# Key pages and new key rows transposed by VectorE in 32x32 blocks, decode rows ordered by groups of four heads

## The chip, the cores and the metric

The kernel runs on one core of a Trainium2 chip. The metric is the device time of one execution in microseconds (us); a time is the median of several runs on the same chip.

## The reference

One inference step of a decoder trunk with two layers. Layer 0 is a conformer convolution, layer 1 is stick-breaking attention; a gated ConvFFN follows each, and a final RMSNorm ends the trunk. There are 512 prompt rows (one new sequence) and 32 decode rows (8 sequences of 4 new tokens). The model width is 1024, in 16 heads of 64. Everything is float32. Each decode sequence has a past of 256 keys and values, which lie in two pages of 128 rows each in a pool of pages; a page table names them. What the change touches is the attention:

```python
def stick_breaking_block(q, k, v, bias, q_start):
    z = jnp.einsum('bqhd,bkhd->bhqk', q, k) * (HEAD_DIM ** -0.5) + bias[None, :, None, None]
    valid = k_pos[None, :] < q_pos[:, None]
    log_fail = jnp.where(valid, jax.nn.log_sigmoid(-z), 0.0)
    after = lax.cumsum(log_fail, axis=3, reverse=True) - log_fail
    weights = jnp.where(valid, jnp.exp(jax.nn.log_sigmoid(z) + after), 0.0)
    return jnp.einsum('bhqk,bkhd->bqhd', weights, v)
...
k_past = jnp.take(cache_k[a], page_table, axis=0)   # 8 sequences x 2 pages x 128 rows x (16 heads x 64)
v_past = jnp.take(cache_v[a], page_table, axis=0)
```

The new keys and values of both prompt and decode rows are outputs as well, one row per token (k_p and v_p for the prompt, k_s and v_s for the decode rows).

## The kernel before

Activations lie transposed in SBUF: 128 channels on the partitions, 8 blocks c of channels, 544 columns (512 prompt rows, then 32 decode rows). Each block holds two heads, one on partitions 0 to 63 and one on 64 to 127. A weight matrix comes in as float32 (raw) and is split into two parts, whi by ScalarE (L398) and wlo by VectorE (L401); activations are split into XH and XL; a product is three matmuls, XH by whi, XL by whi and XH by wlo (in the attention stage L2126, L2127 and L2128). They are called weight matmuls here. In SBUF and PSUM the names are: acc, z, dz, av, one and t are PSUM tiles, the rest is in SBUF.

In the attention stage, about 634 to 834 us of the profile's span, the key and value projections of layer 1 run channel block by channel block (`keys(c, h)` and `values(c, h)`, in two halves h of the columns), and around them goes the attention work of prompt and decode rows. All of it is entered into a list scheduler (`Plan`): each operation is entered with its engine, a cost from a table and what it reads and writes, ranks follow from these, and the scheduler writes out the order of each engine once, when the program is built. On the chip each engine then works through its own order, and waits where an input or a buffer isn't there. When a step moves to another engine or gets another cost, the order around it changes too.

The steps that the change touches:

- **Key pages.** `gather` (L2018): GpSimd issues an indirect DMA per page, 128 rows of 4 KB. Sixteen key pages are gathered and then, into the same buffers, sixteen value pages. The first three are requested before the stage. In `page_logits(m)`, for four pages at a time (m = 0 to 3), PE transposes each page in two groups of four blocks (L2246, into PSUM); one group is copied to SBUF by VectorE, the other by ScalarE (L2253). Pages of the first sequence go into kt, a part of kT's tile, those of the second into two e tiles (`second`).
- **Page logits** (L2264). The decode queries lie in Qz, with two heads in one block of 128 rows (a block-diagonal layout) and 32 columns for each sequence; per m there are 16 matmuls, 32 rows of output by 256 keys. A decode row in these tiles is one of a group g of eight heads.
- **New keys** (`keys`). ScalarE copies the projection into kT (L2164, which also fills kT_s, the decode rows' keys); PE transposes two 128-column blocks per half (L2156), VectorE copies them to kr (L2170), SP stores kr (L2171) in runs of 512 bytes. kr has two buffers. `values` uses the same L2156 for vT.
- **Placing the decode queries.** GpSimd copies qT's decode columns into Qz (L2044, `place_q`, for four sequences at a time) and Qf (L2050), 64 partitions at a time: 2 + 2 and 4 copies.
- **New logits** (L2282): the decode queries Qf by the new keys kT_s, 16 matmuls of 32 by 32. `new_rows` (L2194) transposes the decode rows of k and v for their outputs.
- **Values.** `sequence(n)` (L2326) multiplies the weights of one sequence by its two value pages, 16 matmuls of 32 by 128; the result is added into oacc. `new_values(bg)` adds the new values (L2346, two matmuls of 128 by 128) and transposes oacc (L2351) into dec, the attention output of the decode rows.
- **Prompt attention** uses L2388 (logits), L2394 to L2422 (weights, with scans on VectorE, L2418, and masks on GpSimd, L2402), L2430 and L2450.

SP issues the weight loads and most other DMAs, in one queue in program order.

Of the kernel before, what the change touches and what calls it, by code (L numbers as in the profile page):

```python
# [9 lines left out]
F32 = mybir.dt.float32  # L10
# [240 lines left out]
def tile_trunk(  # L251
# [181 lines left out]
    mnew = base.tile([P, 2, NS], F32, name="mnew")  # L433
    bcol = base.tile([P, 2], F32, name="bcol")
    own = base.tile([P, 4], F32, name="own")
# [4 lines left out]
    oh = base.tile([P, 2, H], F32, name="oh")  # L440
    cb = base.tile([P, 2, NS], F32, name="cb")
    m1 = base.tile([P, NS], F32, name="m1")
    rb = base.tile([P, 2], F32, name="rb")
# [204 lines left out]
    def decode_tables():  # L648
# [6 lines left out]
        dve.tensor_scalar(ti[:, 0:1], pid, 3, 3, op0=ALU.logical_shift_right, op1=ALU.bitwise_and)  # L655
        dve.tensor_scalar(ti[:, 1:2], pid, 3, None, op0=ALU.bitwise_and)
        dve.tensor_scalar(ti[:, 2:3], pid, 5, None, op0=ALU.logical_shift_right)
        dve.tensor_scalar(ti[:, 3:4], pid, 2, 1, op0=ALU.logical_shift_right, op1=ALU.bitwise_and)
        dve.tensor_copy(ti[:, 4:5], pid)
        dve.tensor_copy(tf[:, 0:5], ti[:, 0:5])  # L660
        dve.scalar_tensor_tensor(tf[:, 5:6], tf[:, 2:3], 2.0, tf[:, 3:4], op0=ALU.mult, op1=ALU.add)
        dve.tensor_scalar(cb_i[:, 0, :], t32, 2, None, op0=ALU.logical_shift_right)
# [1918 lines left out]
```

## Time and profile before

| | before |
|---|---|
| median of 3 runs | 1266.06 us (1265.24 to 1266.23) |
| the profiled execution: its own time | 1266.66 us |
| its span | 1265.0 us |
| TensorE clock granted | 0.999 |

The profile is one execution. The span is what the profiler saw from the first to the last instruction, and 1.66 us of the execution's own time lie around it. PE is TensorE's matmuls, PEld its weight loads (they overlap PE), DVE VectorE, ACT ScalarE, POOL GpSimd, SP SyncE; a q behind an engine's name is that engine's DMA issuing. Busy time counts instructions at work; an engine's wait counts only between its instructions. One fp32 matmul shows as two records on PE. Durations of matmuls overlap, since PE is pipelined: what one occupies is read from the distance between starts. A timeline row gives the start in us, the duration, the engine, the line, the operation with its output and inputs, the shapes, and how many instructions stand in the row. A row of a group gives, behind the bar, busy us, mean ns of one, and then the idle time of the engine just before them with what ended it.

### The profile page before, as it was taken

The numbers are of one execution on the slowest core, as the hardware profiler recorded it, in microseconds if no ns is written. First come the engines' busy times: TensorE is split into PE (matmuls) and PEld (weight loads), VectorE is DVE, ScalarE is ACT, GpSimd is POOL, SyncE is SP. The second block draws the span as 40 slices with busy tenths as digits, with TensorE's granted clock in tenths as the row PEclk, the third lists the DMA queues.
The fourth block names the chain that finished last, engine by engine and source line by source line (L and its number), as shares of the span: only waits on it lengthen the run. The fifth ranks groups of instructions, "written<-read, shape, count | busy, mean of one in ns | idle before, by whom it ended". The sixth has DMA issues, their size and how long they took to land.

```text
span 1265.0 us, 26475 instructions
## 1 busy us (share of the span) xinstructions
PE 1253.8 (99%) x10846; PEld 1203.5 (95%) x10846; DVE 1004.6 (79%) x1696; ACT 717.2 (57%) x1436; POOL 165.6 (13%) x291
## 2 busy tenths in 40 slices
PE   9999999999999999999999999999999999999998
PEld 8997699999999999999989888999999999999997
DVE  7999886988987887869865589766988987887863
ACT  6794584646645455445565498754645645454453
POOL 5000014111001000002042143200111001000000
PEclk9999999999999999999999999999999999999999
DMA  7465423123233233244355544342223233232221
GB/s 215 127 172 151 128 68 116 34 85 118 92 98 114 67 119 105 71 144 171 117 183 152 157 139 137 114 148 71 65 87 110 84 110 117 67 118 88 89 77 72
DMA packets 119179, 142.39 MB, mean 113 GB/s; under 512 B 5101, under 2 KB 110245, under 8 KB 118786
## 3 DMA queue, kind: packets, MB, share of 16 engines
q1 hardware_dynamic: 110350, 111.89, 28.4%
q0 software_dynamic: 8704, 28.80, 7.2%
q8 instruction: 85, 1.39, 0.5%
q14 instruction: 36, 0.29, 0.1%
q10 hardware_dynamic: 4, 0.01, 0.0%
HBM read 129.34 MB, written 12.18 MB: 112 GB/s over the span
## 4 chain that ended last, share of the span: by engine, by line
PE 84%; DVE 13%; ACT 1%; issue 1%; DMA 0%; DVEq 0%; ACTq 0%
PE acc L1632 5%; PE acc L1631 5%; PE acc L1630 5%; PE acc L756 4%; PE acc L757 4%; PE acc L758 4%; PE av L893 3%; PE av L1409 3%; PE av L1410 3%; PE av L1411 3%; DVE wlo L401 3%; PE tr L1410 3%; PE tr L1409 3%; PE tr L1411 3%; PE tr L1630 3%; PE tr L1632 2%
## 5 line engine op out<-in xcount | busy, mean ns | idle before, releaser
L398 ACT CAST whi<-raw 128x1024 fp32r<-128x1024 f32 (+2 forms) x247 | 224.2, 911 | 119.4 <-PE av L1410 24.9
L401 DVE TENSOR_TENSOR wlo<-raw,whi 128x1024 fp32r<-128x1024 f32 (+2 forms) x247 | 259.2, 1052 | 26.1 <-ACT whi L398 24.8
L756 PE MATMUL acc<-XH,whi 128*128 128x288 f32 (+1 forms) x384 | 112.7, 294 | 0.0
L758 PE MATMUL acc<-XH,wlo 128*128 128x288 f32 (+1 forms) x384 | 110.3, 287 | 0.9 <-DVE wlo L401 0.9
L757 PE MATMUL acc<-XL,whi 128*128 128x288 f32 (+1 forms) x384 | 110.3, 287 | 0.0
L1409 PE MATMUL av<-HH,whi 128*128 128x288 f32 (+1 forms) x280 | 83.2, 297 | 0.4 <-DVE xT L1719 0.4
L1410 PE MATMUL av<-HL,whi 128*128 128x288 f32 (+1 forms) x280 | 82.6, 295 | 0.0
L1632 PE MATMUL acc<-TH,wlo 128*128 128x272 f32 x288 | 82.6, 287 | 0.0
L1631 PE MATMUL acc<-TL,whi 128*128 128x272 f32 x288 | 82.6, 287 | 0.0
L1630 PE MATMUL acc<-TH,whi 128*128 128x272 f32 x288 | 82.6, 287 | 0.0
L2126 PE MATMUL acc<-XH,whi 128*128 128x256 f32 (+1 forms) x264 | 82.0, 310 | 0.6 <-ACT kT L2164 0.6
L1411 PE MATMUL av<-HH,wlo 128*128 128x288 f32 (+1 forms) x280 | 82.2, 294 | 0.0
L1666 ACT COPY G<-acc 128x272 f32<-128x272 f32 (+1 forms) x72 | 26.8, 372 | 93.9 <-PE acc L1632 93.9
L1409 PE MATMUL tr<-HH,whi 128*128 128x256 f32 (+1 forms) x280 | 78.6, 281 | 0.0
L1410 PE MATMUL tr<-HL,whi 128*128 128x256 f32 (+1 forms) x280 | 78.4, 280 | 0.0
L1411 PE MATMUL tr<-HH,wlo 128*128 128x256 f32 (+1 forms) x280 | 78.3, 280 | 0.0
L2128 PE MATMUL acc<-XH,wlo 128*128 128x256 f32 (+1 forms) x264 | 75.8, 287 | 0.0
L2127 PE MATMUL acc<-XL,whi 128*128 128x256 f32 (+1 forms) x264 | 75.7, 287 | 0.0
L756 PEld LDWEIGHTS acc<-XH,whi 128*128 128x128 f32 x384 | 72.2, 188 | 1.4 <-issue 0.4
L758 PEld LDWEIGHTS acc<-XH,wlo 128*128 128x128 f32 x384 | 72.1, 188 | 1.1 <-DVE wlo L401 1.1
L757 PEld LDWEIGHTS acc<-XL,whi 128*128 128x128 f32 x384 | 72.2, 188 | 0.3
L1570 DVE SCALAR_TENSOR_TENSOR cv<-G,fprm,cv 128x560 f32<-128x560 f32 x88 | 69.5, 797 | 0.5
(465 smaller groups left out, 4373.8 us busy)
## 6 DMA issues: line engine op xcount, KB each, us to landing
raw<-in_ffn_w_gate_dram SPq DMA_DIRECT2D x22, 1024.0 KB
raw<-in_ffn_w_up_dram SPq DMA_DIRECT2D x22, 1024.0 KB, 5.4
raw<-in_ffn_w_down_dram SPq DMA_DIRECT2D x24, 768.0 KB, 4.6
raw<-in_attn_w_qkv_dram SPq DMA_DIRECT2D x12, 1024.0 KB, 5.3
raw<-in_conv_w_in_dram POOLq DMA_DIRECT2D x6, 1024.0 KB, 6.9
rep<-glu SPq DMA_DIRECT2D x36, 142.0 KB, 2.9
raw<-in_conv_w_out_dram POOLq DMA_DIRECT2D x4, 1024.0 KB, 6.0
raw<-in_ffn_w_down_dram SPq DMA_DIRECT2D x8, 512.0 KB
```

What stands on the lines that cost most here:

```text
L398: act.copy(hi[:, k, :], src[:, k])
L401: dve.tensor_tensor(lo[:, k, :], src[:, k], hi[:, k, :], op=ALU.subtract)
L756: pe.matmul(o, hi[:, k, :], XH[:, k, c0:c0 + n], start=(k == 0), stop=False)
L757: pe.matmul(o, hi[:, k, :], XL[:, k, c0:c0 + n], start=False, stop=False)
L758: pe.matmul(o, lo[:, k, :], XH[:, k, c0:c0 + n], start=False, stop=(k == NC - 1))
L1409: pe.matmul(o, hi[:, j + k, :], xh, start=(start and k == 0), stop=False, **kw)
L1410: pe.matmul(o, hi[:, j + k, :], xl, start=False, stop=False, **kw)
L1411: pe.matmul(o, lo[:, j + k, :], xh, start=False, stop=(stop and k == len(xs) - 1), **kw)
L1630: pe.matmul(o, hi[:, j + k, :], xh, start=(start and k == 0), stop=False, **kw)
L1631: pe.matmul(o, hi[:, j + k, :], xl, start=False, stop=False, **kw)
L1632: pe.matmul(o, lo[:, j + k, :], xh, start=False, stop=(k == 3), **kw)
L2126: pe.matmul(o, hi[:, k, :], XH[:, k, c0:c0 + n], start=(k == 0), stop=False)
```

## The change

Key pages and new key rows are no longer transposed on PE. SP now reads the 16 page numbers of the table into registers (`page_numbers`), early in the program, and loads each key page with four DMAs of its own (`key_page`), each with 32 partitions by four runs of 1 KB: partition 32x + p holds, for each quarter q of the page, row 32q + p of the four heads 4x to 4x + 3. One VectorE instruction then transposes the 32x32 blocks of the whole page (128x1024), into kt or an e tile. Value pages stay with GpSimd's indirect DMA. A half of new keys is transposed by one VectorE instruction of 128x256 and stored by four DMAs with runs of 128 bytes.

Channels of key pages stand on the partitions in another order than before: a block k of 32-channel pieces holds one piece of each of the four groups of four heads. So decode rows are ordered by groups of four heads, and everything that meets them changes: Qz becomes 128x1024, GpSimd places queries in sixteen copies of 32 partitions (`place_q`, `place_f`), the new keys' decode columns are copied into the same order (kn, `place_k`, sixteen copies, new), the page logits of the second sequence are 16 matmuls of 128 keys rather than 8 of 256, new logits are two batches of 16 matmuls, the value products 8 matmuls of 256 columns, new values two of 256 columns, and the rows of new keys, new values and the result are turned by matmuls with pieces of the identity. Masks and the logit bias get columns for the new order. The lines of the changed kernel have other numbers: L2145 to L2147 are the weight matmuls, L2282 the page logits, L2264 and L2188 VectorE's transposes, L2417 the prompt's logits, L2061 and L2066 the copies into Qz and Qf, L2296 those into kn, L2431 the masks.

```diff
+            plan.op("sp", 1.0, page_numbers, w=["numbers"])
+            plan.op("dve", 0.6, decode_columns, r=["numbers"], w=["tables"])
+            plan.op("dve", 0.9, decode_masks, r=["tables"])
             for j in range(PAGE_BUFS):
-                plan.op("pool", 1.05, lambda j=j: gather(page_t[j], j, ck), r=["saved", "tables"])
+                plan.op("sp", 2.0, lambda j=j: key_page(page_t[j], j), r=["saved", "numbers"])
...
+    def page_numbers():
+        numbers.extend(nc.sync.value_load(idx[0:1, j:j + 1], min_val=0, max_val=cache_k.shape[1] - 1) for j in range(2 * NB))
+
+    def key_page(t, j):
+
+        pages = cache_k[0, bass.ds(numbers[j], 1)].rearrange("o (q p) (x h) d -> o x p q (h d)", p=32, x=4)
+        for x in range(4):
+            nc.sync.dma_start(out=t[32 * x:32 * x + 32, :].rearrange("p (q r) -> p q r", q=4), in_=pages[0, x])
...
-    Qz = xflat[:, 3 * D:3 * D + NC * 160].rearrange("p (c r) -> p c r", c=NC)
...
-    Qf = dz.tile([P, NC, 2, NS], F32, name="Qf")
+    Qz = xflat[:, 3 * D:4 * D].rearrange("p (k r) -> p k r", k=NC)
+
+    Qf = dz.tile([P, NC, 2 * NS], F32, name="Qf")
     pool.memset(Qz, 0.0)
     pool.memset(Qf, 0.0)
 
...
+    def placed(bg):
+        new = SEQ + 16 * bg
+        for x in range(4):
+            for q in range(4):
+                src = qT[32 * q:32 * q + 32, 2 * x:2 * x + 2, new:new + 16]
+                yield slice(32 * x, 32 * x + 32), x, q, src.rearrange("p c (b i) -> p c b i", b=4)
 
     def place_q(bg):
...
+        for rows, x, q, src in placed(bg):
+            dst = Qz[rows].rearrange("p (c q) (b r) -> p q c b r", q=4, b=4)[:, q, :, :, 4 * x:4 * x + 4]
+            pool.tensor_copy(dst, src)
...
+    def place_f(bg):
+        for rows, x, q, src in placed(bg):
+            dst = Qf[rows].rearrange("p (c q) (b r) -> p q c b r", q=4, b=4)[:, q, :, :, 4 * x:4 * x + 4]
+            pool.tensor_copy(dst, src)
 
     place_q(0)
...
-        rows, src = to_rows(lambda b: kT[:, c, c0 + b * P:c0 + (b + 1) * P], [("k", c, h)])
         kr = sbuf("kr", 2 * P, 2)
-        plan.op("dve", 0.38, lambda: dve.tensor_copy(kr().rearrange("p (b d) -> p b d", b=2), src()), r=[rows], w=[kr])
-        plan.op("sp", 3.0, lambda: nc.sync.dma_start(out=kpv[:, 2 * h:2 * h + 2, c * P:(c + 1) * P],
-                                                     in_=kr().rearrange("p (b d) -> p b d", b=2)), r=[kr])
+        plan.op("dve", 0.15 + 256 * 1.1e-3, lambda: dve.transpose(kr(), kT[:, c, c0:c0 + 256]), r=[("k", c, h)], w=[kr])
+
+        def store():
+            for a in range(4):
+                rows = slice(32 * a, 32 * a + 32)
+                nc.sync.dma_start(out=k_p[0, 0, c0:c0 + 256].rearrange("(b i) h d -> i b (h d)", i=32)[:, :, c * P + 32 * a:c * P + 32 * a + 32],
+                                  in_=kr()[rows].rearrange("i (b j) -> i b j", j=32))
+
+        plan.op("sp", 5.0, store, r=[kr])
...
+            for x in range(4):
+                for j in range(2):
+                    pe.matmul(rows()[HALF[j], x * HD:(x + 1) * HD], src[HALF[j], 2 * x:2 * x + 2, :].rearrange("p c t -> p (c t)"),
+                              ident[HALF[j], HALF[j]], start=(x == 0), stop=(x == 3), skip_group_check=True)
...
+            return t
+        if i < 2 * NB:
+            plan.op("sp", 2.0, lambda: key_page(t(), i), w=[t, ("asked", i)])
         else:
-            plan.op("pool", 1.05, lambda: gather(t(), i % (2 * NB), ck if i < 2 * NB else cv), w=[t, ("asked", i)])
-            plan.op(f"page{i}", 4.0, lambda: None, r=[("asked", i)], w=[(t, 1)])
+            plan.op("pool", 1.05, lambda: gather(t(), i % (2 * NB), cv), w=[t, ("asked", i)])
+        plan.op(f"page{i}", 6.0 if i < 2 * NB else 4.0, lambda: None, r=[("asked", i)], w=[(t, 1)])
...
+                plan.op("pool", 2.4, lambda: place_q(1), w=["Qz"])
         z = zt[bg]
         for odd in range(2):
             for pg in range(2):
                 t = page(4 * m + 2 * odd + pg)
-                for half in range(2):
-                    pt = spare if spare and (odd, pg, half) == (0, 0, 1) else psum("t")
...
-                    def turn(t=t, pt=pt, half=half):
-                        for j in range(4):
-                            c = half * 4 + j
-                            pe.transpose(pt()[:, j * P:(j + 1) * P], t()[:, c * P:(c + 1) * P], ident)
...
-                    plan.op("pe", 0.43, turn, r=[t, (t, 1), "pages"], w=[pt])
-                    eng = ("dve", "act")[half]
...
-                    def keep(pt=pt, half=half, pg=pg, odd=odd, copy=(dve.tensor_copy, act.copy)[half]):
-                        home = second[half]().rearrange("p (c k) -> p c k", c=4) if odd else kt[:, half * 4:half * 4 + 4]
-                        copy(home[:, :, pg * P:(pg + 1) * P], pt().rearrange("p (c k) -> p c k", c=4))
...
-                    plan.op(eng, 0.68 if half == 0 else 0.6, keep, r=[pt], w=[("ktq" if odd else "ktp", 2 * pg + half)],
-                            a=[second[half]] if odd else [])
+
+                def turn(t=t, pg=pg, odd=odd):
+                    dve.transpose(second[pg]() if odd else kt[:, pg * D:(pg + 1) * D], t())
+
+                plan.op("dve", 1.25, turn, r=[t, (t, 1), "pages"], w=[("ktq" if odd else "ktp", pg)],
+                        a=[second[pg]] if odd else [])
 
         def logits():
             for odd in range(2):
                 b = 2 * (m % 2) + odd
...
-        plan.op("pe", 1.72, logits, r=[(k, i) for k in ("ktp", "ktq") for i in range(4)] + ["Qz", *second], w=[z], form="c32")
+                c0 = 32 * b - 16 * odd
+                if odd:
+                    parts = [(pg * P, P, second[pg]()) for pg in range(2)]
+                else:
+                    parts = [(0, KW, kt)]
+                for e in range(2):
+                    for lo, n, src in parts:
+                        keys_of = src.rearrange("p (q k j) -> p k q j", k=NC, j=32)
+                        for u in range(4):
+                            k = 4 * (u % 2) + 2 * (u // 2) + e
+                            pe.matmul(z()[32 * u:32 * u + 32, (m % 2) * KW + lo:(m % 2) * KW + lo + n],
+                                      Qz[:, k, c0:c0 + 32], keys_of[:, k],
+                                      start=(b == e == 0), stop=(b == 3 and e == 1), skip_group_check=True)
...
+    def place_k():
+        for x in range(4):
+            for q in range(4):
+                pool.tensor_copy(kn[32 * x:32 * x + 32].rearrange("p (c q) t -> p q c t", q=4)[:, q], kT_s[32 * q:32 * q + 32, 2 * x:2 * x + 2, :])
+
     def new_logits():
...
+        zn = psum("t")
+        plan.op("pool", 3.0, place_k, r=[("kT_s", c) for c in range(NC)], w=["kn"])
+        for bg in range(2):
+            plan.op("pool", 3.0, lambda bg=bg: place_f(bg), w=["Qf"])
+
+            def f(bg=bg):
+                for v in range(2):
+                    t = 2 * bg + v
+                    for e in range(2):
+                        for u in range(4):
+                            k = 4 * (u % 2) + 2 * (u // 2) + e
+                            pe.matmul(zn()[32 * u:32 * u + 32, t * NS:(t + 1) * NS], Qf[:, k, 32 * v:32 * v + 32], kn[:, k, :],
+                                      start=(t == e == 0), stop=(t == 3 and e == 1), skip_group_check=True)
+
+            plan.op("pe", 0.6, f, r=["Qf", "kn"], w=[zn], form="c32")
...
+            for pg in range(2):
+                values_of = ts[pg]().rearrange("p (x h d) -> p h x d", x=4, h=4)
+                for u in range(4):
+                    pe.matmul(pt()[32 * u:32 * u + 32, :2 * P], wT[:, t, pg, 32 * u:32 * u + 32], values_of[:, 2 * (u % 2) + u // 2],
+                              start=(pg == 0), stop=(pg == 1), skip_group_check=True)
...
+            for v in range(2):
+                pe.matmul(pt()[:, v * KW:(v + 1) * KW], wn[:, 2 * bg + v, :], new_s,
+                          start=(v == 0), stop=True, skip_group_check=True)
 
         def turn():
...
+            first = True
+            for x in range(4):
+                for j in range(2):
+                    for v in range(2):
+                        pick = ident.rearrange("p (j c b x i) -> p j x c b i", j=2, c=2, b=2, x=4)[:, j, x]
+                        home = tr()[HALF[j], :2 * P].rearrange("p (x c v b i) -> p x v c b i", x=4, c=2, v=4, b=2)[:, x, v]
+                        pe.matmul(home, oacc[:, 2 * bg + v, x * HD:(x + 1) * HD], pick, start=(x == v == 0), stop=(x == 3 and v == 1),
...
-        split(hi, lo, dec[rows, :, :, 4 * j:4 * j + 4])
+    split(XH[:, :, SEQ:T], XL[:, :, SEQ:T], dec.rearrange("p c v r -> p c (v r)"))
```

How the orders change, at three places.

PE, in the order before, around the first page logits (L2264; dz is their PSUM tile, xT in L2264 is Qz, kT and the two e tiles hold the transposed pages):

```order
L2246 MATMUL t_8261<-ident,xT 128x128 x4
L2388 MATMUL z_8266<-kT,qT 128x384
L2388 MATMUL z_8268<-kT,qT 128x384
L2388 MATMUL z_8266<-kT,qT 128x128
L2388 MATMUL z_8268<-kT,qT 128x128
L2264 MATMUL dz_8273<-kT,xT 32x256 x8
L2264 MATMUL dz_8273<-e_8192,xT 32x256 x4
L2264 MATMUL dz_8273<-e_8212,xT 32x256 x4
```

And PE in the changed kernel, at its first page logits (L2282):

```order
L2145 MATMUL acc_8411<-XH,whi_8160 128x256
L2146 MATMUL acc_8411<-XL,whi_8160 128x256
L2147 MATMUL acc_8411<-XH,wlo_8161 128x256
L2282 MATMUL dz_8461<-kT,xT 32x256 x8
L2282 MATMUL dz_8461<-e_8324,xT 32x128 x4
L2282 MATMUL dz_8461<-e_8403,xT 32x128 x4
L2282 MATMUL dz_8461<-e_8324,xT 32x128 x4
L2282 MATMUL dz_8461<-e_8403,xT 32x128 x4
```

The page transposes between the weight matmuls are gone, and the page logits stand right behind weight matmuls.

GpSimd before, in the last third of the stage (L2402 are the prompt's masks, L2018 gathers of value pages):

```order
L2402 AFFINE_SELECT e_9882<-e_9882 128x2x128
L2018 DMA xT<-in_cache_v_dram,idx 128x1024
L2402 AFFINE_SELECT e_9988<-e_9988 128x2x128 x2
L2018 DMA xT<-in_cache_v_dram,idx 128x1024 x2
L2402 AFFINE_SELECT e_10204<-e_10204 128x2x128 x2
```

GpSimd in the changed kernel, there:

```order
L2431 AFFINE_SELECT e_9980<-e_9980 128x2x128 x2
L2032 DMA xT<-in_cache_v_dram,idx 128x1024
L2296 COPY kn<-kT_s 32x2x32 x16
L2431 AFFINE_SELECT e_10172<-e_10172 128x2x128 x2
L2066 COPY Qf<-qT 32x2x4x4 x16
L2431 AFFINE_SELECT e_10470<-e_10470 128x2x128
```

The sixteen copies into kn and the second sixteen into Qf come between the masks; the first batch of new logits reads kn, the second reads kn and the second half of Qf.

VectorE before, shortly ahead of the stage (L1490, L1486, L1372 and L1868 belong to the queries' projection):

```order
L1490 TENSOR_TENSOR TLq<-kT,THq 128x2x272 x2
L1868 SCALAR_TENSOR_TENSOR qT<-acc_7815,qT 128x272
L1486 TENSOR_TENSOR kT<-kT,XH 128x544
L401 TENSOR_TENSOR wlo_7829<-raw_7390,whi_7828 128x1024
L1372 TENSOR_TENSOR Sq<-raw_7390 128x1024
```

VectorE in the changed kernel, there (the same steps are L1493, L1871, L1489, L401 and L1375):

```order
L1493 TENSOR_TENSOR TLq<-kT,THq 128x2x272 x2
L2264 STREAM_TRANSPOSE kT<-xT 128x1024
L1871 SCALAR_TENSOR_TENSOR qT<-acc_7975,qT 128x272
L1489 TENSOR_TENSOR kT<-kT,XH 128x544
L401 TENSOR_TENSOR wlo_7989<-raw_7541,whi_7988 128x1024
L1375 TENSOR_TENSOR Sq<-raw_7541 128x1024
```

The first page's transpose stands ahead of the next weights' low part; the second and third follow a few instructions later, still ahead of the stage.

More of the change, by code (lines that the diff above doesn't have):

```diff
@@ L2260, in logits @@
                 b = 2 * (m % 2) + odd
-                for g in range(2):
-                    for s in range(4):
-                        c = 4 * g + s
-                        pe.matmul(z()[32 * s:32 * s + 32, g * KW:(g + 1) * KW], Qz[:, c, 32 * b:32 * b + 32], turned(odd, c),
-                                  start=(b == 0 and g == 0), stop=(b == 3), skip_group_check=True)
-        plan.op("pe", 1.72, logits, r=[(k, i) for k in ("ktp", "ktq") for i in range(4)] + ["Qz", *second], w=[z], form="c32")
+                c0 = 32 * b - 16 * odd
[11 more added lines that the diff above has]
+                                      start=(b == e == 0), stop=(b == 3 and e == 1), skip_group_check=True)
+        plan.op("pe", 1.72, logits, r=[(k, i) for k in ("ktp", "ktq") for i in range(2)] + ["Qz", *second], w=[z], form="c32")
         if m % 2:
@@ L2321, in f @@
         def f():
-            for g in range(2):
-                for pg in range(2):
-                    for s in range(4):
-                        c = 4 * g + s
-                        pe.matmul(pt()[32 * s:32 * s + 32, g * P:(g + 1) * P], wT[:, 2 * bg + g, pg, 32 * s:32 * s + 32],
-                                  ts[pg]()[:, c * P:(c + 1) * P], start=(g == pg == 0), stop=(pg == 1), skip_group_check=True)
-        plan.op("pe", 0.9, f, r=[*ts, *((t, 1) for t in ts), ("wT", 2 * bg), ("wT", 2 * bg + 1), "pages"], w=[pt], form="c32")
@@ L2349, in turn @@
         def turn():
-            for g in range(2):
-                pe.transpose(t()[:, g * P:(g + 1) * P], o[:, g * P:(g + 1) * P], ident)
-        plan.op("pe", 0.45, new, r=["new", "pages", ("wn", 2 * bg)], w=[pt])
-        for g in range(2):
-            cols = slice(g * P, (g + 1) * P)
-            plan.op("dve", 0.25, lambda g=g, cols=cols: dve.scalar_tensor_tensor(
-                o[:, cols], o[:, cols], nsn[:, 2 * bg + g:2 * bg + g + 1], pt()[:, cols], op0=ALU.mult, op1=ALU.add),
-                r=[pt, "nsn"], w=[("oacc", bg)])
@@ new lines, in new_values @@
+        plan.op("pe", 0.9, new, r=["new", "pages", ("wn", 2 * bg)], w=[pt])
+        for v in range(2):
+            t = 2 * bg + v
+            plan.op("dve", 0.37, lambda v=v, t=t: dve.scalar_tensor_tensor(
+                oacc[:, t, :], oacc[:, t, :], nsn[:, t:t + 1], pt()[:, v * KW:(v + 1) * KW], op0=ALU.mult, op1=ALU.add),
+                r=[pt, "nsn"], w=[("oacc", t)])
+        plan.op("pe", 1.0, turn, r=[("oacc", 2 * bg), ("oacc", 2 * bg + 1)], w=[tr], form="c64")
+        plan.op("act", 0.3, lambda: act.copy(dec[:, :, 2 * bg:2 * bg + 2, :], tr()[:, :2 * P].rearrange(
+            "p (c v r) -> p c v r", c=NC, v=4)[:, :, 0:2, :]), r=[tr], a=["dec"])
@@ L2489, in tile_trunk @@
         if c == 5:
[L2490 removed]
+            new_rows(kT_s, [("kT_s", i) for i in range(NC)], ksv)
             new_logits()
```

122 lines of the change are left out of this document (43 added, 79 removed).

## The prediction

> **What bounds the kernel now.** I read the page's busy times first, then the busy time in the stretches that the change touches (the attention stage, about 634 to 834 us of the span), then the waits of PE there.
>
> ```profile
> PE 1253.8 (99%) x10846; PEld 1203.5 (95%) x10846; DVE 1004.6 (79%) x1696; ACT 717.2 (57%) x1436; POOL 165.6 (13%) x291
> ```
>
> Busy time by stretch; the columns are the stretch, its length, the busy us (and instructions) of PE, PEld, DVE, ACT and POOL, the granted TensorE clock, the DMA share and GB/s:
>
> ```profile
> 598.00:626.00 28.00, 28.00 (x224) 28.00 (x223) 27.86 (x40) 16.82 (x28) 3.32 (x2) 1.00 0.30 90
> 636.00:712.00 76.00, 76.00 (x684) 68.95 (x682) 42.03 (x59) 38.42 (x68) 21.04 (x25) 1.00 0.60 184
> 634.00:834.00 200.00, 198.95 (x2006) 176.16 (x2004) 145.36 (x212) 139.54 (x248) 57.97 (x67) 1.00 0.47 147
> ```
>
> All the waits of PE from 560 to 860 us (us in total, times, longest):
>
> ```profile
> PE acc L2126 <- ACT kT L2164: 0.6, 1, 0.6
> PE av L1630 <- ACT qT L1866: 0.5, 1, 0.5
> PE tr L1746 <- DVE sqa L1806: 0.4, 1, 0.4
> PE one L2156 <- DVE kr L2170: 0.4, 1, 0.4
> ```
>
> PE is busy 198.95 of 200 us at a granted clock of 1.00, and waits 1.9 us in all over three hundred. So PE's queue is the bound, and each matmul taken out of it shortens the run by what it occupies there, until some other engine answers late. VectorE has 55 us left in the stage, ScalarE 60, GpSimd 142.
>
> **What PE loses.** 16 pages of 8 transposes (L2246, issued in groups of four) and 16 key halves of 2 (L2156 on kT) go: 160 instructions. Their mean durations overlap each other, so I take the distance between starts. First a group of four among weight matmuls (L2126 to L2128), then a pair; then the two groups of the stage:
>
> ```profile
> 653.29 0.60 PE L2246 MATMUL t<-ident,xT 128*128 128x128 f32 x4
> 653.65 0.36 PE L2126 MATMUL acc<-XH,whi 128*128 128x256 f32 x1
> 653.85 0.28 PE L2127 MATMUL acc<-XL,whi 128*128 128x256 f32 x1
> 653.97 0.28 PE L2128 MATMUL acc<-XH,wlo 128*128 128x256 f32 x1
> ...
> 748.74 0.38 PE L2156 MATMUL one<-ident,kT 128*128 128x128 f32 x2
> 748.88 0.38 PE L2126 MATMUL acc<-XH,whi 128*128 128x288 f32 x1
> 749.10 0.29 PE L2127 MATMUL acc<-XL,whi 128*128 128x288 f32 x1
> 749.23 0.29 PE L2128 MATMUL acc<-XH,wlo 128*128 128x288 f32 x1
> ```
>
> ```profile
> L2246 PE MATMUL t<-ident,xT 128*128 128x128 f32 x124 | 18.9, 275 | 0.0
> L2156 PE MATMUL one<-ident,kT 128*128 128x128 f32 x32 | 6.1, 272 | 0.0
> ```
>
> From 653.29 to 653.85 is 0.56 us, of which the first weight matmul is 0.12 (653.85 to 653.97): 0.44 for four. From 748.74 to 749.10 is 0.36, less 0.13: 0.23 for two. (The group shows 124 of the 128 page transposes; the first four went to another buffer.) Removed: 32 × 0.44 + 16 × 0.22 = 14.1 + 3.5 = **17.6 us**.
>
> **What PE gains.** No added form stands in the trace, so each is bounded by its neighbours, again from start to start:
>
> ```profile
> 648.67 1.14 PE L2388 MATMUL z<-kT,qT 64*128 64x384 f32 x8
> 649.73 1.07 PE L2264 MATMUL dz<-kT,xT 128*32 128x256 f32 x16
> 650.62 1.05 PE L2264 MATMUL dz<-e,xT 128*32 128x256 f32 x16
> ...
> 807.60 0.46 PE L2282 MATMUL one<-kT_s,Qf 128*32 128x32 f32 x32
> 807.88 1.10 PE L2326 MATMUL dz<-xT 128*32 128x128 f32 x32
> 808.91 0.38 PE L2126 MATMUL acc<-XH,whi 128*128 128x256 f32 x1
> ...
> 829.54 0.61 PE L2346 MATMUL dz<-xT,wn 128*128 128x128 f32 x4
> 829.91 0.36 PE L2126 MATMUL z<-XH,whi 128*128 128x256 f32 x1
> ```
>
> One fp32 matmul shows as two records here. 32 records of 32 columns take 0.28, 32 of 128 columns 1.03, 16 of 256 columns 0.89, four wide ones of 128 columns 0.37. The new logits become two such batches: +0.28. The eight value products become 16 records of 256: 0.89 against 1.03, say −0.06 each, −0.5 (−1.0 to 0). The second half of the page logits becomes 32 records of 128 columns, +0.1 in each of four (0 to +0.14). The matmuls of the new values get twice as wide, at two places: +0.37 each (0 to 0.74 of doubt). The transposes of the result (two of them, 0.22 by the pair above) become 16 matmuls of 64 rows, at two places: between 0.28 and 1.03, so +0.4 each (0.1 to 0.8). The new rows (two transposes) become 8 matmuls, also at two: half of that, +0.1 each (−0.1 to 0.3). Sum +0.28 − 0.5 + 0.4 + 0.74 + 0.8 + 0.2 = **+1.9 us** (−0.7 to +4). Net on PE: −15.7.
>
> **VectorE.** It loses 16 copies of a page half and 16 of a key half, and gets 16 transposes of 128x1024 and 16 of 128x256. ScalarE loses its 16 page copies, which lay beside PE. A transpose doesn't stand in the trace; its nearest rows are passes from SBUF to SBUF:
>
> ```profile
> L401 DVE TENSOR_TENSOR wlo<-raw,whi 128x1024 fp32r<-128x1024 f32 x35 | 42.9, 1228 | 1.8 <-ACT whi L398 1.4
> L2407 DVE TENSOR_SCALAR e<-e 128x1024 f32<-128x1024 f32 x20 | 13.8, 690 | 6.2 <-POOL e L2402 6.2
> L2418 DVE TENSOR_TENSOR_SCAN s<-ones,s 128x512 f32<-128x512 f32 x16 | 19.0, 1230 | 1.0 <-ACT s L2409 0.9
> L2253 DVE COPY e<-t 128x512 f32<-128x512 f32 x8 | 5.5, 691 | 7.9 <-PE t L2246 7.8
> L2170 DVE COPY kr<-one 128x256 f32<-128x256 f32 x16 | 6.7, 418 | 13.8 <-PE one L2156 13.8
> ```
>
> So a page's transpose lies between 0.69 us and 2.46 (the scan's 1.23 for 512, doubled); I take 1.23, one pass at the speed of the two-input subtraction and of the half-page copy (0.69 for 512), and 0.42 for a key half. By the order three page transposes stand ahead of 634 us. The stage then has 145.4 − 11.0 − 6.7 + 13 × 1.23 + 16 × 0.42 = 150 us of VectorE in some 184. In the crowded part, 636 to 712, where nearly all pages are turned, it is 42.0 − 11.0 − 2.5 + 16.0 + 2.5 = 47 in the 62 us that are left of the 76 when 14.1 are gone: it fits, and I charge nothing. The first transpose stands where VectorE has no gap (27.86 of 28.00 us from 598 to 626); 1.2 us more before its weights there can show on PE, 0 to 1 us, taken 0.
>
> **GpSimd.** Eight copies of decode rows become 80 small ones (32 partitions), and PE now waits for two batches that did not exist. What a small copy costs, and what can hold it:
>
> ```profile
> 631.59 0.63 POOL L2044 COPY xT<-qT 64x128 f32<-64x128 f32 x2 [30.27 <-ACT qT L1866]
> 632.28 3.24 POOL L2050 COPY Qf<-qT 64x128 f32<-64x128 f32 x4
> ```
>
> ```profile
> 632.92 2.44 DVE L401 TENSOR_TENSOR wlo<-raw,whi 128x1024 fp32r<-128x1024 f32 x2
> ```
>
> ```profile
> L2050 POOL COPY Qf<-qT x4: 288/743/1341, 632.3 to 634.3; 64x128 f32<-64x128 f32 x4
> ```
>
> ```profile
> L1580 POOL COPY SF<-G x44: 204/213/732, 234.7 to 1168.3; 128x16 f32<-128x16 f32 x44
> ```
>
> The short copy (L1580, 16 elements) takes 0.21 at the median; the four of L2050 take from 0.29 to 1.34 us, and the long ones stand beside the two subtractions that VectorE begins at 632.92: each waited for one to end. The Trainium skill, "SBUF — State Buffer", section "SBUF: two separate sides", says that a VectorE operation with two SBUF inputs and a GpSimd one lock each other out for the whole instruction. The trace agrees (1.34 against 0.29), and the rule speaks against this change: by it, with the pair taken all the time, the sum would be that of rival (a).
>
> So: 0.21 to 0.25 per copy, and up to 1.2 for one that meets a subtraction. The first 32 (about 8 us, 11 with holds) begin at 631.6, and the first page logits, at 649.73 today, come only about 2 us earlier: no stall. The second batch of Qz has a page's time. The new keys' 16 copies (kn) take 3.4 to 4.0, with one hold 4.6 to 5.2; PE has, by the order, 22 weight matmuls (2.7), a value product (0.9), a logits group (1.06, 648.67 to 649.73) and the new rows (0.5) meanwhile, 5.2 less the time that ScalarE needs to copy the last key columns out: I charge 0.8. Qf's second 16 stand behind kn and two masks; 4.0, the masks' 1.4 and a hold are 6.6 against 30 weight matmuls, a logits group and the first batch (4.9): 1.6. Together **+2.4 us** (0 to 8).
>
> **SP and the DMAs.** Sixteen reads of page numbers stand on SP's queue, nine ahead of the two loads at 30.45:
>
> ```profile
> 10.04 2.10 SPq L697 DMA_DIRECT2D xs<-in_x_sample_dram  x1
> 30.45 0.83 SPq L1099 DMA_DIRECT2D scr<-in_state_conv_dram  x2
> ```
>
> SP has nothing to do from 12.1 to 30.45, up to 2 us for each of the nine; taken 0 (to +3, as the table itself must land first). The loads behind the page DMAs are weights, asked for far ahead. The stores of new keys get runs of 128 bytes, 16,384 packets in place of 4,096:
>
> ```profile
> q1 hardware_dynamic: 110350, 111.89, 28.4%
> out_dram<-kr SPq DMA_DIRECT2D x16, 128.0 KB, 1.9
> ```
>
> That queue's packet of some 1 KB takes 0.284 × 16 × 1265 / 110350 = 52 ns. A key half comes every 11 us or so and puts 64 packets on each engine: 3.3 us at 52 ns, where a share of 0.47 leaves 5.8. Taken 0. The Trainium skill, "DMA: Bandwidth & Descriptors", section "Specifications", says that a transfer under 512 bytes makes the engine read, modify and write; by that a packet would cost more than its bytes, and no row here has such packets in number. That is rival (c).
>
> **The sum.** The profiled run took 1266.66 (span 1265.0, 1.66 around it), 0.6 above the median of 1266.06. 1266.66 − 15.7 + 2.4 = 1253.4; less 0.6, and rounded, **1253 us**.
>
> **The rivals.**
> (a) GpSimd's copies are held all through, 0.5 to 0.6 us each: kn and Qf take 8 to 10 us each instead of 4, and PE waits 8 us and not 2.4. For it: three of the four L2050 copies took 0.74 or more. Against: VectorE does a two-input pass from SBUF only some of the time. About 1259.
> (b) Slower: VectorE becomes the bound because a transpose runs at the scan's pace, 2.46 a page and 0.67 a half. From 636 to 712 that is 42.0 − 13.5 + 32 + 4 = 64.5 us in 62; VectorE was idle 34 of 76 there waiting for inputs, and if a third of this stays, PE waits 11 + 2.5, and 2 more at the first transpose: 1253 + 15.5 = about 1269. It decides from about 2.3 us a page; below 1.7 nothing shows. Against it: a transpose has no carry from element to element.
> (c) Slower too: 128-byte packets at 200 ns. 64 of them are 12.8 us where 5.8 are free; kr has two buffers, so the queues fill, weights come late by up to 16 × 7 = 112 us less their lead: 1280 or more. It decides from about 90 ns a packet.
> (d) No change: the transposes at about 2 us and (a) together eat the gain: 1266.
> (e) The added forms and Pool cost nothing: 1266.06 − 17.6 − 0.7 = 1248.
>
> **How the numbers follow.** My own case (1249 to 1257) 0.68, (a) 0.14, (b) 0.07, (c) 0.03, (d) 0.04, (e) 0.04. Left out of 1248 to 1263 are (b), (c), (d) and half of (e): 0.16. A measurement can tell 0.2%, 2.5 us. Faster is 0.68 + 0.14 + 0.04 = 0.86, same 0.04, slower 0.10.
>
> **What would show it.** L2246's rows gone and PE busy about 16 us less; a page transpose near 1.2 us; no wait of PE before the page logits; waits of PE for Pool's kn and Qf before the new logits of 1 to 4 us in all; DMA share up by less than 0.1. Wrong if PE waits for VectorE before the page logits, or for weights.

## The result, and the profile after

| | before | changed |
|---|---|---|
| median of 6 runs | 1265.82 us | 1257.06 us (1256.80 to 1257.69) |
| the profiled execution, its span | 1266.66, 1265.0 us | 1257.69, 1255.8 us |

The ratio is 0.9932, 95% interval 0.9919 to 0.9945: 8.8 us faster, where 13 were forecast. The time lies in the range that was given, 4.1 us above the forecast itself and at the upper edge of the prediction's own case (1249 to 1257).

The page's busy times after, then the same three stretches as before (28, 76 and 200 us; PE, PEld, DVE, ACT, POOL, clock, DMA share, GB/s):

```profile
PE 1241.5 (99%) x10742; PEld 1188.2 (95%) x10742; DVE 1010.8 (80%) x1699; ACT 707.9 (56%) x1421; POOL 172.2 (14%) x347
```

```profile
598.00:626.00 28.00, 27.27 (x216) 27.05 (x216) 27.83 (x39) 16.54 (x27) 11.08 (x21) 1.00 0.34 83
636.00:712.00 76.00, 76.00 (x739) 68.22 (x738) 61.03 (x80) 43.60 (x77) 15.07 (x30) 1.00 0.74 181
634.00:834.00 200.00, 198.70 (x2010) 172.91 (x2009) 153.72 (x219) 135.72 (x245) 58.31 (x100) 1.00 0.55 153
```

PE's busy time fell by 12.3 us and PE is still the bound. VectorE in the crowded part went from 42 to 61 us of 76 and PE still did not wait there. From 598 to 626, where PE had been busy all the time, it now misses 0.73 us.

All waits of PE from 560 to 860 us after:

```profile
PE t L2310 <- POOL Qf L2066: 0.8, 1, 0.8
PE acc L1633 <- ACT qT L1869: 0.7, 1, 0.7
PE av L1633 <- ACT qT L1869: 0.5, 1, 0.5
PE tr L1749 <- DVE sqa L1809: 0.4, 1, 0.4
PE av L2479 <- ACT e L2462: 0.3, 1, 0.3
```

Two of the old waits went (0.6 and 0.4, for kT and kr), and three came: 0.8 for GpSimd's Qf before the second batch of new logits, 0.7 for queries at 619 us, and 0.3 for e.

Three matmuls that stand at the same places of PE's order in both kernels, first before, then after: one near 598 us, the one behind the wait of 0.49 that both have near 629, and the first behind the stage.

```profile
599.17 0.29 PE L1409 MATMUL acc<-XH,whi 128*128 128x288 f32 x1
629.24 0.40 PE L1630 MATMUL av<-XH,whi 128*128 128x272 f32 x1 [0.49 <-ACT qT L1866]
844.03 0.30 PE L495 MATMUL acc<-XH,whi 128*128 128x288 f32 x1
```

```profile
598.76 0.29 PE L1412 MATMUL acc<-XH,whi 128*128 128x288 f32 x1
629.82 0.40 PE L1633 MATMUL av<-XH,whi 128*128 128x272 f32 x1 [0.49 <-ACT qT L1869]
832.40 0.29 PE L497 MATMUL acc<-XH,whi 128*128 128x288 f32 x1
```

From the second to the third it is 214.8 us before and 202.6 after: the stage gains 12.2 us. From the first to the second it is 30.1 and 31.1: ahead of the stage 1.0 us is lost.

Groups of VectorE's transposes in the changed kernel:

```profile
L2264 DVE STREAM_TRANSPOSE e<-xT 128x1024 f32<-128x1024 f32 x8 | 9.8, 1230 | 0.4 <-DMA xT<-in_cache_k_dram 0.4
L2188 DVE STREAM_TRANSPOSE kr<-kT 128x256 f32<-128x256 f32 x16 | 6.9, 434 | 9.1 <-DMA out_dram<-kr 6.3 <-ACT kT L2183 2.8
```

A page takes 1.23 us (the eight that go into kT as well) and a key half 0.43; the prediction took 1.23 and 0.42. Timeline rows of PE's new forms (each up to the start of the row below it):

```profile
783.34 0.68 PE L2219 MATMUL one<-ident,kT_s 64*64 64x64 f32 x16
783.95 0.39 PE L2145 MATMUL acc<-XH,whi 128*128 128x256 f32 x1
```

```profile
786.27 0.46 PE L2310 MATMUL t<-kn,Qf 128*32 128x32 f32 x32
786.66 1.13 PE L2417 MATMUL z<-kT,qT 64*128 64x512 f32 x4
```

```profile
791.97 0.32 PE L2310 MATMUL t<-kn,Qf 128*32 128x32 f32 x12
793.07 0.38 PE L2310 MATMUL t<-kn,Qf 128*32 128x32 f32 x20 [0.79 <-POOL Qf L2066]
793.38 0.44 PE L2175 MATMUL one<-ident,vT 128*128 128x128 f32 x2
```

```profile
817.43 1.03 PE L2370 MATMUL dz<-xT,wn 128*128 128x256 f32 x4
818.39 2.40 PE L2479 MATMUL av<-e,vtok 128*64 128x128 f32 x40
820.63 1.11 PE L2380 MATMUL one<-ident,Zd 128*64 128x16 f32 x32
821.53 1.56 PE L2479 MATMUL av<-e,vtok 128*64 128x128 f32 x24
822.87 1.11 PE L2380 MATMUL one<-ident,Zd 128*64 128x16 f32 x32
823.91 0.66 PE L2459 MATMUL t<-ident,e 128*128 128x128 f32 x4
```

New rows take 0.61 us, a batch of new logits 0.39 and 0.62 (without its wait), new values up to 0.96, the transposes of the result 0.90 and 1.04. GpSimd's copies, by line (shortest, median and longest in ns):

```profile
L2066 POOL COPY Qf<-qT x32: 199/206/1197, 604.4 to 791.9; 32x32 f32<-32x32 f32 x32
```

```profile
L2296 POOL COPY kn<-kT_s x16: 227/231/1278, 774.7 to 784.7; 32x64 f32<-32x64 f32 x16
```

The median is the free price of 0.2 us, the longest are the held ones; the mean is 0.41 for Qf and 0.44 for kn. The two batches that PE waits for, as they stand on GpSimd's timeline:

```profile
774.66 0.75 POOL L2296 COPY kn<-kT_s 32x64 f32<-32x64 f32 x1
777.97 6.96 POOL L2296 COPY kn<-kT_s 32x64 f32<-32x64 f32 x15 [2.56 <-DMA xT<-in_cache_v_dram,idx]
786.74 6.28 POOL L2066 COPY Qf<-qT 32x32 f32<-32x32 f32 x16 [0.97 <-PE t L2310]
```

The copies into kn take 7.7 us and the second sixteen into Qf 6.3.

One change was not foreseen: the end. The last instructions of GpSimd and SP, first after, then before (a row gives shortest, median and longest in ns, and the first and last start):

```profile
L2603 POOLq DRAIN  x3: 46/109/6687, 1248.3 to 1255.6; - x3
L2603 SPq DRAIN  x3: 7/7/7, 1253.0 to 1255.3; - x3
```

```profile
L2577 POOLq DRAIN  x3: 46/103/3092, 1259.5 to 1264.7; - x3
L2577 SPq DRAIN  x3: 7/7/7, 1264.1 to 1264.4; - x3
```

At the end all engines drain and meet. Before, SP came last, at 1264.2, when the final stores had landed; GpSimd's drain had ended at 1262.5. After, SP comes at 1253.0, and GpSimd's drain, 6.69 us long and begun at 1248.3, ends at 1255.0: the other engines wait 2.0 us for it. From the end of PE's last matmul to the end of the span it is 5.8 us before and 7.8 after.

### The profile page after: what moved, and what is told of

The parts are those of the page before. It is cut to its first block, busy times and chain, and to the rows that moved or that the text cites. A ratio compares the mean times of both kernels' runs of the same rounds, so it can differ in the third digit from the quotient of the medians.

```text
span 1255.8 us, 26647 instructions
## 1 busy us (share of the span) xinstructions
PE 1241.5 (99%) x10742; PEld 1188.2 (95%) x10742; DVE 1010.8 (80%) x1699; ACT 707.9 (56%) x1421; POOL 172.2 (14%) x347
## 5 line engine op out<-in xcount | busy, mean ns | idle before, releaser
L401 DVE TENSOR_TENSOR wlo<-raw,whi 128x1024 fp32r<-128x1024 f32 (+2 forms) x247 | 258.7, 1050 | 29.6 <-ACT whi L398 28.1
L2145 PE MATMUL acc<-XH,whi 128*128 128x256 f32 (+1 forms) x264 | 80.1, 303 | 0.0
L2147 PE MATMUL acc<-XH,wlo 128*128 128x256 f32 (+1 forms) x264 | 75.7, 287 | 0.0
```

The source lines that it names most:

```text
L401: dve.tensor_tensor(lo[:, k, :], src[:, k], hi[:, k, :], op=ALU.subtract)
L2145: pe.matmul(o, hi[:, k, :], XH[:, k, c0:c0 + n], start=(k == 0), stop=False)
```

## The experiments

The theory after the result: PE's queue did lose what was forecast, and four terms took some of it back: PE's new forms cost twice the estimate, the first page's transpose makes PE wait, so does GpSimd for Qf, and GpSimd's drain sets the end. The rival: VectorE's load or the 128-byte stores ate the difference. The table compares each kernel with the kernel before measured beside it on the same chip; the changed kernel stands at −8.8 and, measured again, at −9.1.

| kernel | median, us | minus before | ratio (95%) |
|---|---|---|---|
| rows on PE | 1260.30 | −6.2 | 0.9950 (0.9936 to 0.9964) |
| first page later | 1256.28 | −10.2 | 0.9920 (0.9906 to 0.9934) |
| pages twice | 1268.22 | +1.8 | 1.0011 (1.0002 to 1.0020) |
| copies twice | 1266.94 | +0.5 | 1.0006 (0.9997 to 1.0015) |
| tiny DMAs | 1254.74 | −11.4 | 0.9910 (0.9895 to 0.9925) |
| state rows on SP | 1254.72 | −11.4 | 0.9912 (0.9897 to 0.9928) |
| copies on VectorE | 1257.03 | −9.1 | 0.9930 (0.9916 to 0.9944) |
| rows alone | 1265.37 | −0.8 | 0.9992 (0.9983 to 1.0001) |
| changed again | 1257.46 | −9.1 | 0.9929 (0.9916 to 0.9943) |
| later and SP | 1255.06 | −11.5 | 0.9910 (0.9895 to 0.9925) |
| later and tiny | 1253.75 | −12.8 | 0.9904 (0.9889 to 0.9919) |
| before and tiny | 1267.06 | +0.5 | 1.0006 (0.9996 to 1.0016) |

**Rows on PE**, the second part undone.

```diff
-        plan.op("dve", 0.15 + 256 * 1.1e-3, lambda: dve.transpose(kr(), kT[:, c, c0:c0 + 256]), ...
-        plan.op("sp", 5.0, store, r=[kr])
+        rows, src = to_rows(lambda b: kT[:, c, c0 + b * P:c0 + (b + 1) * P], [("k", c, h)])
+        plan.op("dve", 0.38, lambda: dve.tensor_copy(kr()..., src()), r=[rows], w=[kr])
+        plan.op("sp", 3.0, lambda: nc.sync.dma_start(out=kpv[...], in_=kr()...), r=[kr])
...
```

> The changed kernel with the new key rows as they were before: PE transposes each key half (16 pairs), VectorE copies them, SP stores runs of 512 bytes. The theory (PE's queue is the bound, a pair occupies 0.22 us on it): 16 x 0.22 = 3.5 us longer than the changed kernel's 1257.1, so 1260 to 1261. The rival (the 128-byte stores or VectorE's 128x256 transposes hold something up, and part of the missing 4 us lies there): less than 1.5 us longer, or no change; GpSimd's last drain stays at 6.7 us by both.

It came out 2.6 to 3.0 us longer than the changed kernel, each set against the kernel before (3.3 between the two profiled runs, 3.4 in the stage alone, between the same two matmuls as above). The pairs' time on PE is real, and neither the stores nor VectorE hold PE back.

**Rows alone**, the second part without the first.

> The kernel before, with the new key rows alone changed (VectorE's 128x256 transposes, stores of 128-byte runs, key pages as before). The theory (PE's queue): 16 x 0.22 = 3.5 us shorter than before, 1262 to 1263; GpSimd's last drain 3.1 us. The rival (the 128-byte stores cost, or the pair's time on PE is filled by something else): 1265 to 1266.

A miss: 0.8 us, and the interval holds no change. The pairs are gone, but the new order brought two waits, PE's longest from 560 to 860 us in that run:

```profile
PE acc L2126 <- ACT kT L2164: 1.9, 1, 1.9
PE acc L495 <- DVE xT L2539: 1.0, 1, 1.0
```

The first stood at 0.6 before, the second did not exist. In the two profiles, the same step is worth 3.4 us of the stage in one order and 1 us in the other.

**First page later.**

```diff
+                if (m, odd, pg) == (0, 0, 0):
+                    plan.op("act", 0.2, lambda: act.copy(kt[:, 0:1], qT[:, NC - 2, 0:1]), w=["pages"])
```

> The changed kernel, with the first page's transpose held back by a one-column copy on ScalarE that needs a late block of the queries, so that it stands behind the weights' low parts near 627 us and no longer at 614. The theory (the transpose at 614 pushed VectorE's gapless stretch back by 1.2 us and PE waited 0.9 for it near 619): 0.7 to 1.2 us shorter than 1257.1, PE's gap of 0.73 near 619 gone. The rival (PE's gap near 619 comes from GpSimd's copies, which now stand there too, or the delay only moves to 629): within 0.3 us of 1257.1.

1.1 to 1.4 us shorter, and the wait at 619 is gone; PE in the 28 us up to 625, which answer to 598 to 626:

```profile
597.00:625.00 28.00, 28.00 (x224) 28.00 (x223) 27.86 (x39) 17.25 (x29) 16.90 (x21) 1.00 0.27 78
```

GpSimd's copies still stand there (16.9 us of them), so they were not the cause. The first transpose was: from the matmul at 598 to the one at 629 it takes 30.1 us again, as in the kernel before, and 31.0 or 31.1 in every run that leaves the first transpose where it was. So its price is 1.0 us; the medians' 1.1 to 1.4 hold other differences too.

**Pages twice** and **copies twice**.

```diff
-                    dve.transpose(second[pg]() if odd else kt[:, pg * D:(pg + 1) * D], t())
+                    for _ in range(2 if 4 * m + 2 * odd + pg >= PAGE_BUFS else 1):
+                        dve.transpose(second[pg]() if odd else kt[:, pg * D:(pg + 1) * D], t())
```

> The changed kernel, with each of the 13 later key pages transposed twice by VectorE (the same into the same place), 13 x 1.23 = 16.0 us more on VectorE, as if a page cost 2.46. The theory (VectorE had room, 61 of 76 us between 636 and 712): it now has 77 of 76, so PE waits for a part of it, 3 to 9 us longer. The rival (b) of the prediction as it was worked out: 13 to 16 us longer. No effect at all would say that VectorE's waits there were all soft.

```diff
-        for x in range(4):
+        for x in (0, 0, 1, 1, 2, 2, 3, 3):
...
-            plan.op("pool", 3.0, lambda bg=bg: place_f(bg), w=["Qf"])
+            plan.op("pool", 3.0, lambda bg=bg: [place_f(bg) for _ in range(1 + bg)], w=["Qf"])
```

> The changed kernel, with GpSimd's copies into kn and the second sixteen into Qf made twice (32 more copies, at the 0.39 to 0.44 us that they take some 13 us more). The theory (GpSimd's two batches are just covered by PE's other work, 0.8 us of wait for Qf, and more would show in full): 9 to 13 us longer. The rival (PE has other work to take first, GpSimd is off the path): under 3 us longer. GpSimd's last drain: 6.7 us if it hangs on the DMAs it issued, longer if it hangs on the number of its copies.

Pages twice is 10.5 to 10.9 us longer than the changed kernel, between the two expectations, so both missed; copies twice is 9.2 to 9.6 longer, in the theory's 9 to 13, but not by waits alone. PE's rows with their waits, of pages twice and then of copies twice:

```profile
662.91 1.12 PE L2460 MATMUL t<-ident,e 128*128 128x128 f32 x4 [2.08 <-DVE e L2453]
678.85 0.66 PE L2460 MATMUL t<-ident,e 128*128 128x128 f32 x4 [2.73 <-DVE e L2453]
698.12 0.63 PE L2460 MATMUL t<-ident,e 128*128 128x128 f32 x4 [1.45 <-DVE e L2453]
```

```profile
788.72 0.26 PE L2310 MATMUL t<-kn,Qf 128*32 128x32 f32 x4 [2.60 <-POOL kn L2296]
800.67 0.30 PE L2310 MATMUL t<-kn,Qf 128*32 128x32 f32 x4 [3.85 <-POOL Qf L2066]
```

The waits shown are 6.3 us in the one and 6.5 in the other (with two small ones, copies twice has 7.0, and 0.8 of them the changed kernel has too). The rest stands elsewhere. Between 650 and 710 us PE falls back 9.8 us against the changed kernel's profile in pages twice, and 9.8 between 775 and 805 in copies twice; so some 3.5 us are missing in both. They stand in the clock (the figure behind the five engines' busy times), of pages twice:

```profile
697.00:701.00 4.00, 2.88 (x24) 2.91 (x25) 3.97 (x5) 1.32 (x4) 1.83 (x1) 1.00 0.56 153
662.90:666.30 3.40, 3.39 (x12) 2.72 (x14) 3.37 (x4) 1.19 (x2) 0.58 (x2) 0.50 0.03 6
679.90:683.30 3.40, 3.40 (x18) 3.38 (x17) 3.37 (x5) 1.56 (x5) 0.00 (x0) 0.51 0.88 167
```

and of copies twice:

```profile
790.50:793.90 3.40, 3.40 (x15) 2.52 (x12) 2.28 (x5) 1.06 (x1) 2.88 (x10) 0.50 0.03 5
800.70:804.10 3.40, 3.18 (x42) 2.91 (x43) 2.01 (x7) 0.62 (x2) 0.60 (x3) 0.50 0.00 0
```

After waits of 2.08, 2.73, 2.60 and 3.85 us the granted clock was 0.50 for 3.4 us, beginning at once or up to 1.8 us after the wait's end. PE was busy nearly all of that time, so half of it, 1.7 us of work, is an estimate of what each one lost. After 1.45 (and after 1.51 in copies on VectorE and 1.93 in rows alone) the clock stayed at 1.00. With 2 × 1.7 the sums are 6.3 + 3.4 = 9.7 and 7.0 − 0.8 + 3.4 = 9.6, where 9.8 was measured in both. The median of pages twice holds differences between executions as well: its runs lie from 1266.23 to 1268.68, and the profile is of the fastest.

GpSimd's two batches got 9.5 us longer in copies twice (11.65 for 6.96 and 11.08 for 6.28); 6.2 of this shows as waits of PE. That the time grew by as much as was added is partly luck, through the clock.

**Copies on VectorE.**

```diff
-        plan.op("pool", 3.0, place_k, r=[("kT_s", c) for c in range(NC)], w=["kn"])
+        plan.op("dve", 1.7, place_k, r=[("kT_s", c) for c in range(NC)], w=["kn"])
...
-            plan.op("pool", 3.0, lambda bg=bg: place_f(bg), w=["Qf"])
+            plan.op(("pool", "dve")[bg], (3.0, 1.7)[bg], lambda bg=bg: place_f(bg), w=["Qf"])
```

> The changed kernel, with the sixteen copies into kn and the second sixteen into Qf made by VectorE in place of GpSimd. The theory (at 0.39 to 0.44 us a copy GpSimd's two batches cost PE the 0.8 us wait for Qf): 0.5 to 1 us shorter, 1256 to 1256.6, no wait of PE for kn or Qf. The rival (VectorE is full there as well and the wait moves to it): 1257 or more.

No change: the rival was right. The wait for Qf is gone; PE waits in its place for the new logits' sum on VectorE, and 0.4 us in all for kn, which VectorE now makes:

```profile
PE t L2459 <- DVE Zn L2315: 1.5, 1, 1.5
```

**GpSimd's drain**: tiny DMAs and state rows on SP, then both with the first page later, and the kernel before with tiny DMAs.

```diff
+    tiny = scratch.tile([P, 16], F32, name="tiny")
+    for j in range(16):
+        pool.dma_start(out=tiny[0:4, j:j + 1], in_=Qf[0:4, 0, j:j + 1])
```

```diff
-                    pool.dma_start(out=dst[:, fs].rearrange("r (f c) -> r f c", f=nk),
+                    nc.sync.dma_start(out=dst[:, fs].rearrange("r (f c) -> r f c", f=nk),
```

> The changed kernel, with 16 tiny DMAs more that GpSimd issues ahead of the attention stage (a few floats each into a scratch tensor that nothing reads), so that GpSimd issues 84 DMAs, as in the kernel before, and not 68. If GpSimd's last drain hangs on the number of DMAs it has issued, it takes 3.1 us as before and not 6.7, and the end comes 1.9 us earlier: 1255 to 1255.5. If it hangs on the indirect gathers, on their bytes, or on GpSimd's copies: 6.7 us and no change from 1257.1.

> The changed kernel, with the 16 stores of the ConvFFN state rows issued by SP and no longer by GpSimd (52 DMAs of GpSimd's in place of 68; its last DMA is then a gather of a value page near 770 us, not a store near 1205). If the last drain waits on what the late stores left behind, it falls to 1 to 3 us and the end comes 2 us earlier, 1255 to 1255.5, unless weights behind those stores on SP's queue come late. If it hangs on the number of DMAs: some other length than 6.7; on the copies: 6.7.

> The changed kernel once more, beside the next ones on the same chip: 1257 within 0.7, GpSimd's last drain 6.69 us.

> The changed kernel with the first page's transpose behind the weights' low parts (as in the run with the later first page) and the state rows' stores on SP (as in the run with them there). The theory (the two losses lie at different places and add): 1.2 + 2 us shorter than the changed kernel in the same call, 1253.5 to 1254.5. The rival (one hides behind the other): 1255 or more.

> The changed kernel with the first page's transpose later and the 16 tiny DMAs of GpSimd. The theory: 1253.5 to 1254.5, GpSimd's drain 2 us and no longer the last to come. If the drain hangs on the moment and not on the DMAs issued before it: some other length.

> The kernel before with 16 tiny DMAs of GpSimd more (100 in place of 84). If more DMAs make the last drain shorter: under 3 us. If its length just follows where in some count the last DMA falls: any other length between 1 and 7 us; over 4.7 us it would show as a later end, up to 2 us, and under that the time stays at 1266.

The drains, in this order: tiny DMAs, state rows on SP, later and tiny, before and tiny, copies twice:

```profile
L2606 POOLq DRAIN  x3: 46/109/1949, 1248.0 to 1253.2; - x3
```

```profile
L2603 POOLq DRAIN  x3: 46/109/5381, 1246.7 to 1252.6; - x3
```

```profile
L2608 POOLq DRAIN  x3: 46/109/1954, 1246.4 to 1251.7; - x3
```

```profile
L2580 POOLq DRAIN  x3: 46/102/3424, 1259.2 to 1264.5; - x3
```

```profile
L2603 POOLq DRAIN  x3: 46/109/6691, 1257.4 to 1264.6; - x3
```

Twice the copies leave it at 6.69; other DMAs of GpSimd's change it, to 1.95 and 5.38, and kernels with the same DMAs repeat it to 0.01 us. So it hangs on the DMAs that GpSimd issued, and the time fell by 2.3 to 2.7 us in both. The length doesn't grow or shrink with their number (52: 5.38, 68: 6.69, 84: 3.09 or 1.95, 100: 3.42); by what rule it goes stays open.

Not all of that fall is the drain. From the end of PE's last matmul to the end of the span it is 7.8 us in both profiles of the changed kernel, 5.8 with tiny DMAs and 6.5 with state rows on SP: 2.0 and 1.3 us. Another 0.4 to 0.5 us is a wait of PE for ScalarE near 1000 us, which both profiles of the changed kernel have and no other profile has; why stays open.

Later and tiny is 3.7 us faster than the changed kernel measured beside it (1253.75 against 1257.46) and the fastest of all: there both gains are had, 1.0 of the first page and 2.0 of the drain, and the wait near 1000 us is gone. Later and SP, at 1255.06, missed the theory's numbers by half a us and stands on the rival's side, but its trace doesn't show the rival's mechanism. From the matmul at 598 to the one at 629 it takes 30.1 us and state rows on SP 31.1, so the first page's gain is there. In the two profiles other differences hide it: the matmul at 598 stands at 599.13 in later and SP and at 598.00 in state rows on SP, though the program is the same up to there, and 0.4 us more is lost near 770. The 1.1 us arise in the first 25 us of the execution. The two profiles of the changed kernel differ there by 0.7 us, without a wait of PE that would account for it, so half a us between medians of four runs cannot be told from this.

## Why the prediction was right, and where it was off

It was right in the bound, the sign and the range; the forecast was 4.1 us too low. By its own steps:

| term, us | forecast | measured |
|---|---|---|
| transposes off PE, with the two waits that went | −17.6 | −17.2 (the remainder) |
| PE's new forms | +1.9 | +3.9 |
| GpSimd's batches | +2.4 | +0.8 |
| a new wait for e in the stage | not seen | +0.3 |
| the stage, sum of these | −13.3 | −12.2 |
| first transpose at 614 | 0 (0 to 1) | +1.0 |
| the wait near 1000 us | not seen | +0.5 |
| GpSimd's drain at the end | not seen | +2.0 |
| sum | −13.3 | −8.7; the span shows −9.1 (1255.83 less 1264.97) |

The stage and the first transpose are measured between the same matmuls of both profiles, the end from PE's last matmul on. The 0.4 us between the sum and the span is how far the two executions differ up to 598 us (598.76 and 599.17).

- **What PE loses** was right, as far as it can be told: 12.2 of the stage, the new forms' 3.9, and the new waits' 1.1 give 17.2. This is a remainder and no measurement of its own. Rows on PE confirms the smaller part, 3.4 for 3.5.
- **What PE gains** was mis-sized. New logits +0.73 (0.39 + 0.62 − 0.28; forecast 0.28), new rows +0.4 twice (0.61 less 0.22; forecast 0.1), transposes of the result +1.5 (0.90 + 1.04 less two pairs; forecast 0.8), new values +0.9 (forecast 0.74); page logits (forecast +0.4) and value products (forecast −0.5) nothing. The measured sum still lies in the bounds of −0.7 to +4, at their upper end: the forms with 64 rows took 0.028 to 0.038 us a record, at or over the upper neighbour's 0.032 (1.03 for 32), where the middle between 0.009 and 0.032 had been taken.
- **VectorE** was right: 1.23 and 0.43 us, 154 of 200 us in the stage, no wait of PE in the crowded part. Only the first transpose, where the prediction saw VectorE without a gap and still took 0 of its 0 to 1, cost 1.0.
- **GpSimd** came out at +0.8 for +2.4 by two errors that cancel, which is luck. The copies cost more: kn took 7.7 us where 3.4 to 5.2 was expected, close to rival (a)'s 8 to 10, and Qf's second sixteen 6.3 where 4.0 and a hold was. But PE had more to do meanwhile: from kn's first copy at 774.66 to the first batch at 786.27 it is 11.6 us, where the prediction counted 5.2, so kn was done by 784.9 and PE didn't wait for it at all, and 0.8 us for Qf. Rival (a)'s copies came by more than half, its 8 us of waits did not. What the Trainium skill, "SBUF — State Buffer", section "SBUF: two separate sides", says of the lock between VectorE operations with two SBUF inputs and GpSimd goes with these rows. Of the 80 small copies 55 took 0.20 to 0.26 us and 25 took over 0.4; all 25 stand beside a VectorE operation with two inputs, while 19 of the short ones lie wholly beside one of its transposes, which did not hold them.
- **SP and the DMAs** cost PE nothing, as forecast. SP's loads of the state rows went out at 30.13 us. In the trace the 16,384 packets of 128 bytes took 13 ns each, and packets of 512 bytes 28, far below the 90 ns from which rival (c) would decide; so it is out. What the Trainium skill, "DMA: Bandwidth & Descriptors", section "Specifications", says of transfers under 512 bytes, that they are read, modified and written, doesn't show in the kernel's time; the 128-byte packets took nearly twice as long per byte as those of 512. The stores do hold VectorE: it waited 6.3 us in all for kr's stores to land (row L2188 above), and PE did not. The DMA share rose by 0.08 in the stage as forecast (under 0.1), but by 0.14 in the crowded part.
- **Rival (b)** did not come, as a page takes 1.23. Its price was too high: without the first transpose it had 13.5 us of waits (with slower key halves), and with 13 pages at 2.46 the kernel takes 10.5 to 10.9 us more, 6.3 of them waits and some 3.4 two clock stretches. That this ends at 1268.2, where 1269 was worked out, is luck, as the changed kernel itself is 4 us slower than forecast.
- **The sum** lacked a place: the end. The prediction followed PE and the engines beside it up to the stage's end and has no term for what comes after; that GpSimd's drain at the end had only 1.7 us of cover before (1264.2 less 1262.5) stood in the trace and was not read.
- **The signs**: L2246's rows are gone, a page takes 1.23 and PE doesn't wait before the page logits. PE's busy time fell by 12.3 and not by about 16, and the waits for kn and Qf are 0.8, below the 1 to 4.

## What to carry to other kernels

Taking work off a PE-bound queue pays what its start-to-start distances say, if what takes its place is counted form by form from a neighbour with as few columns. A step that moves to an engine with room on average still costs where that engine has no gap, so the place in the order counts and not the share. Read the last microseconds too: which engine arrives last, and by how much the others are covered.

## What was not expected of the hardware

- GpSimd's last drain takes 1.95 to 6.69 us in these runs, the same to 0.01 for the same DMAs, and can be what the end waits for.
- PE's granted clock fell to 0.50 for 3.4 us after each of the four waits of 2.08 us or more between matmuls, and after none of up to 1.93. The Trainium skill, "TensorE: Matmul & The Clock Gate", section "Why this matters for your kernels", gives gaps of some 3 us as the limit; three of the four here were shorter, and the measurement decides.
- Two executions of the changed kernel differed by 0.7 us within PE's first 25 us, and those of its variants by up to 1.4, with the same waits of PE; why stays open.
